# Ordering the splitting of weights behind the instructions that empty PSUM

## The chip, the cores and the metric

The kernel runs on one core of one Trainium2 chip. The metric is the device time of one execution in microseconds (us). Three runs of the kernel before took 2464.74, 2468.38 and 2469.51 us; their median is 2468.38. One more execution was recorded by the profiler, and all times inside the kernel come from that one.

TensorE (PE) multiplies matrices, VectorE (DVE) and ScalarE (ACT) work on tiles elementwise, SyncE (SP) issues the transfers. Each works through a queue of its own in order; engines wait for one another by semaphores.

## The reference

One layer of a streaming encoder for 256 frames of width 2048, in float32: a gated feed-forward block, a mixer of two attentions, a cross attention to 256 memory tokens with 4 heads of width 512, and a second feed-forward block. Each is followed by a layer norm of the scaled input plus the block's output. Cut to what matters here:

```python
def swiglu_ffn(x, w_in, w_out):
    g, u = jnp.split(x @ w_in, 2, axis=-1)
    return (jax.nn.silu(g) * u) @ w_out

def hybrid_mixer(u, ...):
    proj = u @ w_in                      # q, k, v of A; latents of B; two gates
    y_a = chunked_relbias_attention(q_a, k_a, v_a, rel_bias) @ w_o_a   # 16 heads of 64
    y_b = mla_attention(q_lat, kv_lat, ..., cos, sin) @ w_o_b          # 16 heads, rotary part
    return (g_a * y_a + g_b * y_b) @ w_out

def memory_cross_attention(h, mem, ...):
    k, v = split((layer_norm(mem) @ w_xkv))
    return softmax((h @ w_xq) @ k.T / sqrt(512)) @ v @ w_xo
```

Nearly all of the work is matrix products of 256 rows with large weights, each of which is read from memory once.

## The kernel before, in words

**Two halves.** Every float32 operand is split in two parts that TensorE multiplies at its faster format: hi, a rounded copy, and lo, the rest. A product is hi by both halves of the input plus lo by its hi half. For weights this is done on the chip: a raw weight tile of 128 x 2048 comes by one transfer of 1 MB (line 191), ScalarE rounds it in two casts of 1024 columns (`halves`, line 262), and VectorE subtracts (line 265). There are three buffers each for raw, hi and lo. Inputs are split the same way (lines 253 and 254).

**Units.** `run` walks a list of units, each of which multiplies one weight tile. Before it writes the instructions of unit i, it writes loading and splitting for the weights ahead, up to `UNITS` = 2 units ahead. The order in which the instructions finally stand in each engine's queue is made by the scheduler, which goes by priorities (mostly the order of writing) and by what an instruction depends on; `issue_after(x)` adds that an instruction stands behind x in its engine's queue.

**What empties PSUM.** There are four banks for results of the kind `mm` and four of the kind `at`. A wide unit (`mm_wide`, lines 275 and 277) has 16 matmuls of hi into 512 columns and 16 of lo into 256. Its result is added up by `total`: ScalarE copies the upper half (line 283), VectorE adds the lower (line 284). The feed-forward blocks and the larger projections (line 309, and line 363 for those with sums of weights, which lines 246 and 248 form on VectorE) use a scheme with fewer products, whose results are combined by `shared`: two copies on ScalarE (lines 674 and 675) and four operations on VectorE (676 to 679).

**Softmax.** In the attentions VectorE adds the bias (line 1055) and finds the maxima (824), ScalarE takes exponentials (827), VectorE normalizes (831). The result is transposed by a transfer: ScalarE sorts the bytes into planes (841), SP issues the transfer, ScalarE joins the planes again (849). `join` has the order "behind `next_hi`", the last cast of the next weight. Lines 1028 and 1082/1083 are the scores and the outputs of an attention; 973 scales a transposed input.

Of the kernel before, what the change touches and what calls it, by code (L numbers as in the profile page):

```python
# [14 lines left out]
ALU = mybir.AluOpType  # L15
# [4 lines left out]
S = 256  # L20
# [53 lines left out]
class Act:  # L74


    def __init__(self, blocks):
        self.blocks = blocks
# [21 lines left out]
class Kernel:  # L100
    def __init__(self, ctx, tc, t, out):
        self.tc, self.nc, self.t, self.out = tc, tc.nc, t, out

        def pool(name, bufs=1, **kw):
            return ctx.enter_context(tc.tile_pool(name=name, bufs=bufs, **kw))

        self.const = pool("const")
        self.wraw = pool("wraw", 3)
        self.whi = pool("whi", UNITS + 1)
        self.wlo = pool("wlo", UNITS + 1)  # L110
        self.blocks = pool("blocks")
        self.res = pool("res")
        self.work = pool("work", 4)
        self.small = pool("small", 4)
        self.ps_mm = pool("ps_mm", 4, space=PSUM)
        self.ps_at = pool("ps_at", 4, space=PSUM)
        self.items = []
        self.uid = 0
        self.chain = self.sent = self.last_hi = self.ln_act = None
        self.cut = self.early = False  # L120


    def name(self, s):
# [128 lines left out]
    def split(self, src, hi, lo):  # L252
        copied = self.nc.scalar.copy(hi, src)
        self.nc.vector.tensor_tensor(lo, src, hi.bitcast(F32), ALU.subtract)
        return copied

    def halves(self, src, hi, lo):

        n = src.shape[1]
        for c in range(0, n, 1024):  # L260
            d = min(c + 1024, n)
            self.last_hi = self.nc.scalar.copy(hi[:, c:d], src[:, c:d])  # L262

        with self.tc.issue_after(self.chain.ins) if self.chain is not None else nullcontext():
            self.last_lo = self.nc.vector.tensor_tensor(lo[:, :n], src, hi[:, :n].bitcast(F32), ALU.subtract)  # L265
        return hi, lo

# [11 lines left out]
    def total(self, ps, out=None, scale=1.0):  # L279

        t = self.w1()
        if scale == 1.0:
            self.nc.scalar.copy(t, ps[:, S:])
            self.nc.vector.tensor_tensor(t if out is None else out, t, ps[:, :S], ALU.add)  # L284
        else:
            self.nc.scalar.mul(t, ps[:, S:], scale)
            self.nc.vector.scalar_tensor_tensor(t if out is None else out, ps[:, :S], scale, t, ALU.mult, ALU.add)
        return t

    def mm_tok(self, ps, tt, w, x, kts, start, stop, c=0, m=512):  # L290
# [325 lines left out]
    def out_pair(self, bank, src, g, nk, x, at, fx, scale, st, sums_in=SUM_HOME):  # L616

        nc, h = self.nc, self.h
        ps, qs = {}, {}

        def shared():
            for (tt, a), s in qs["add"].items():
                c = (2 * g + a) * 512
                hs = h[tt][:, c:c + 512]
                if scale:
                    nc.vector.scalar_tensor_tensor(hs, hs, ALPHA, s, ALU.mult, ALU.add)
                else:
                    nc.vector.tensor_tensor(hs, hs, s, ALU.add)

        def finish():  # L630
            for tt in range(2):
                for a in range(2):
                    self.finish(tt, 2 * g + a, ps[tt, a], scale and not at, st)
        self.pair_group(bank, src, 512, nk, x, at, fx, ps, qs, shared, sums_in)
        self.add(finish)
# [33 lines left out]
    def shared(self, qs, n):  # L669

        nc = self.nc
        a, b, u, c = (self.w2()[:, :n] for _ in range(4))
        q = [qs[i][:, :n] for i in range(4)]
        nc.scalar.copy(a, q[0])
        nc.scalar.copy(b, q[1])
        nc.vector.tensor_tensor(u, a, q[2], ALU.add)
        nc.vector.tensor_tensor(b, b, u, ALU.subtract)
        nc.vector.tensor_tensor(u, u, q[3], ALU.add)
        nc.vector.tensor_tensor(c, b, q[3], ALU.subtract)  # L679
        qs["add"] = {(0, 0): a, (0, 1): b, (1, 0): u, (1, 1): c}  # L680

    def first_group(self, tag, xT, before, ps, fx):
# [1088 lines left out]
```

## Time and profile before

| | us |
|---|---|
| median of three runs | 2468.38 |
| lowest, highest run | 2464.74, 2469.51 |
| the profiled execution | 2465.43 |
| its span (first to last instruction) | 2463.7 |
| TensorE busy | 2430.7 |
| VectorE busy | 2121.4 |
| ScalarE busy | 1545.9 |

The profiled execution is 1.7 us longer than its span and 2.95 us below the median of the runs. In the lines of the waits, an engine, line and tile wait for another engine's line; behind the colon stand the sum in us, how many times, and the longest. In the timeline a row has the start, the duration of the group, the engine, line, operation and tiles, the number of instructions in the group (x), and in brackets how long the engine was idle before and what ended it. Rows of the windows have, for each engine, busy us and instructions in that stretch, and then the granted clock of TensorE, the share of the transfer engines in use, and GB/s. Instructions on an engine overlap a little: from one start to the next is some 0.1 us less than the duration.

### The profile page before, as it was taken

The page shows a single profiled execution, that of the slowest core. Times are in us where ns is not written, and L with a number is a line of the kernel's source. Part 1 is how long each engine was busy: PE and PEld are TensorE (multiplying, and loading weights), DVE is VectorE, ACT ScalarE, POOL GpSimd, SP SyncE. Part 2 cuts the span into 40 slices and gives each one's busy share as a digit, 9 for nine tenths or more (in the row PEclk, how much of TensorE's full clock was granted, in tenths as well). Part 3 has the DMA queues.
Part 4 walks back from the last instruction along what each step waited for, and adds up shares of the span by engine and source line. Part 5 has one row for each costly group of instructions (what it writes and reads, how often), then busy time and mean ns, then how long its engine had stood idle before and what let it go on. Part 6 is the DMA issues. An engine that isn't in the chain of part 4 may idle for free.

```text
span 2463.7 us, 29637 instructions
## 1 busy us (share of the span) xinstructions
PE 2430.7 (99%) x11286; PEld 2028.2 (82%) x11286; DVE 2121.4 (86%) x2423; ACT 1545.9 (63%) x2017; POOL 36.2 (1%) x81
## 2 busy tenths in 40 slices
PE   9999999999999999989999999999999999999999
PEld 8888888888888888878888887888888888887887
DVE  8999989889788897689788789869879999888896
ACT  6676655667455557778565686656566665556662
POOL 0000000000000001000000000000000000000000
PEclk9999999999999999999999999999999999999999
DMA  7766665656646656676676567555556666566564
GB/s 262 253 218 216 203 212 209 221 193 216 233 169 214 213 205 207 221 198 183 206 250 228 180 219 227 196 175 206 188 196 212 220 212 219 206 213 214 179 229 163
DMA packets 176415, 516.20 MB, mean 210 GB/s; under 512 B 111728, under 2 KB 112496, under 8 KB 121104
## 3 DMA queue, kind: packets, MB, share of 16 engines
q1 hardware_dynamic: 170816, 495.83, 59.8%
q0 software_dynamic: 4592, 17.30, 2.3%
q8 instruction: 88, 1.44, 0.2%
q10 hardware_dynamic: 864, 1.18, 0.1%
q14 instruction: 55, 0.45, 0.1%
HBM read 485.30 MB, written 2.10 MB: 198 GB/s over the span
## 4 chain that ended last, share of the span: by engine, by line
PE 74%; DVE 9%; ACT 8%; DMA 5%; issue 3%; SPq 0%; DVEq 0%; ACTq 0%
PE at L309 21%; PE mm L309 20%; PE mm L363 8%; PE at L363 8%; PE mm L296 8%; PE mm L275 4%; DVE lo L265 3%; ACT hi L262 3%; DMA raw<-ffn_w_in 2%; PE mm L277 2%; ACT w L849 1%; PE at L1028 1%; ACT X L262 1%; DMA raw<-w_xv 1%; DMA w<-w 0%
## 5 line engine op out<-in xcount | busy, mean ns | idle before, releaser
L262 ACT CAST hi<-raw 128x1024 fp32r<-128x1024 f32 (+1 forms) x852 | 804.3, 982 | 540.0 <-PE at L309 113.9
L265 DVE TENSOR_TENSOR lo<-raw,hi 128x2048 fp32r<-128x2048 f32 (+1 forms) x427 | 902.6, 2115 | 174.0 <-ACT hi L262 163.1
L309 PE MATMUL mm<-hi,T 128*128 128x512 f32 (+1 forms) x1328 | 311.7, 385 | 5.8 <-DVE w L679 4.6
L309 PEld LDWEIGHTS mm<-hi,T 128*128 128x128 f32 x1328 | 247.2, 188 | 54.8 <-DVE w L679 6.5
L309 PE MATMUL at<-hi,T 128*128 128x512 f32 x1152 | 275.4, 390 | 0.6 <-DVE w L679 0.6
L309 PEld LDWEIGHTS at<-hi,T 128*128 128x128 f32 x1152 | 215.8, 188 | 47.2 <-DVE w L679 2.4
L265 DVE TENSOR_TENSOR X<-H,X 128x2048 fp32r<-128x2048 f32 (+1 forms) x83 | 186.7, 2250 | 37.7 <-ACT X L262 37.7
L262 ACT CAST X<-H 128x1024 fp32r<-128x1024 f32 (+1 forms) x166 | 169.7, 1034 | 74.5 <-DVE H L248 48.0
L309 PE MATMUL mm<-lo,T 128*128 128x512 f32 (+1 forms) x664 | 160.6, 384 | 0.0
L309 PEld LDWEIGHTS mm<-lo,T 128*128 128x128 f32 x664 | 124.5, 189 | 23.1
L309 PE MATMUL at<-lo,T 128*128 128x512 f32 x576 | 142.6, 389 | 0.0
L309 PE MATMUL at<-hi,H 128*128 128x512 f32 x560 | 133.4, 390 | 0.1
L309 PEld LDWEIGHTS at<-lo,T 128*128 128x128 f32 x576 | 108.1, 188 | 22.4
L309 PE MATMUL mm<-hi,H 128*128 128x512 f32 x480 | 118.6, 398 | 6.1 <-DVE w L284 3.1
L309 PEld LDWEIGHTS at<-hi,H 128*128 128x128 f32 x560 | 104.9, 188 | 22.2 <-DVE w L679 0.6
L248 DVE TENSOR_TENSOR H<-H,raw 128x512 f32<-128x512 f32 (+1 forms) x166 | 112.4, 677 | 1.6
L309 PEld LDWEIGHTS mm<-hi,H 128*128 128x128 f32 x480 | 91.5, 192 | 26.6 <-DVE w L679 4.2
L246 DVE TENSOR_TENSOR H<-raw 128x1024 f32<-128x1024 f32 (+1 forms) x83 | 99.6, 1200 | 1.7 <-DMA raw<-ffn_w_in 0.9
L363 PE MATMUL mm<-X,X 128*128 128x512 f32 x342 | 90.2, 389 | 0.0
L262 ACT CAST X<-raw 128x1024 fp32r<-128x1024 f32 (+1 forms) x54 | 54.9, 1034 | 56.3 <-DVE raw L248 25.8
L363 PE MATMUL at<-X,X 128*128 128x512 f32 (+1 forms) x315 | 82.1, 385 | 3.5 <-ACT X L262 3.5
L849 ACT COPY w<-w 128x1024 uint16<-128x1024 uint16 (+1 forms) x60 | 73.6, 1270 | 7.3 <-DMA w<-w 7.3
(373 smaller groups left out, 4120.0 us busy)
## 6 DMA issues: line engine op xcount, KB each, us to landing
raw<-ffn_w_in SPq DMA_DIRECT2D x150, 1024.0 KB, 4.9
raw<-ffn_w_out SPq DMA_DIRECT2D x66, 1024.0 KB, 4.9
raw<-w_gate SPq DMA_DIRECT2D x32, 1024.0 KB, 4.8
raw<-ffn_w_out_r SPq DMA_DIRECT2D x16, 1024.0 KB, 5.1
raw<-w_qk SPq DMA_DIRECT2D x16, 1024.0 KB, 5.5
raw<-w_o_b SPq DMA_DIRECT2D x16, 1024.0 KB, 4.8
raw<-w_out SPq DMA_DIRECT2D x16, 1024.0 KB, 5.5
raw<-w_xk SPq DMA_DIRECT2D x16, 1024.0 KB, 5.5
```

What stands on the lines that cost most here:

```text
L246: self.nc.vector.tensor_tensor(two[0], two[1], raw[:, :m].unsqueeze(1).to_broadcast([P, 2, m]), ALU.add)
L248: self.nc.vector.tensor_tensor(t[:, a * m:a * m + m], t[:, b * m:b * m + m], raw[:, a * m:a * m + m], ALU.add)
L262: self.last_hi = self.nc.scalar.copy(hi[:, c:d], src[:, c:d])
L265: self.last_lo = self.nc.vector.tensor_tensor(lo[:, :n], src, hi[:, :n].bitcast(F32), ALU.subtract)
L275: self.nc.tensor.matmul(ps, hi[j], x.both(kt), start=(j == 0), stop=False)
L277: self.last_mm = self.nc.tensor.matmul(ps[:, :S], lo[j], x.at(0, kt), start=False, stop=(j == n - 1))
L296: self.last_mm = self.nc.tensor.matmul(ps, x.at(xi, kt)[:, tt * P:(tt + 1) * P], w[wi][:, j * 512 + c:j * 512 + c + m], start=(start and j ...
L309: self.last_mm = self.nc.tensor.matmul(ps[tt, g][:, :n], x.at(xi, kt)[:, tt * P:(tt + 1) * P], w[wi][:, c:c + n], start=first and j + wi + ...
L363: self.last_mm = self.nc.tensor.matmul(bank[:, :m], a[xi], v[wi][:, c * m:(c + 1) * m], start=own and first and wi + xi == 0, stop=own and ...
L849: self.nc.scalar.copy(self.words(u, n).rearrange("p (c k) -> p k c", k=2), self.words(s, n).rearrange("p (k c) -> p k c", k=2))
L1028: nc.tensor.matmul(ps[:, c0:c0 + nk], q[:, tt * P:(tt + 1) * P], k[:, :nk], start=(j == 0), stop=(j == len(parts) - 1))
```

## The change

`total` and `shared` now remember their last ScalarE and VectorE instruction (`evicted`). `halves` puts the two casts behind the remembered ScalarE instruction, and the subtraction behind the remembered VectorE instruction, in these engines' queues. No instruction is added, removed or altered. The lines of the helpers move: a cast of a weight is line 268 after, a subtraction 272, the copy and add of a total 290 and 291, the four steps of `shared` 684 to 687, the join 857.

```diff
@@ -118,6 +118,7 @@
         self.uid = 0
         self.chain = self.sent = self.last_hi = self.ln_act = None
         self.cut = self.early = False
+        self.evicted = {}
 
 
     def name(self, s):
@@ -254,14 +255,20 @@
         self.nc.vector.tensor_tensor(lo, src, hi.bitcast(F32), ALU.subtract)
         return copied
 
+    def after_out(self, engine):
+        last = self.evicted.get(engine)
+        return self.tc.issue_after(last.ins) if last is not None else nullcontext()
+
     def halves(self, src, hi, lo):
 
         n = src.shape[1]
-        for c in range(0, n, 1024):
-            d = min(c + 1024, n)
-            self.last_hi = self.nc.scalar.copy(hi[:, c:d], src[:, c:d])
-
-        with self.tc.issue_after(self.chain.ins) if self.chain is not None else nullcontext():
+        with self.after_out("act"):
+            for c in range(0, n, 1024):
+                d = min(c + 1024, n)
+                self.last_hi = self.nc.scalar.copy(hi[:, c:d], src[:, c:d])
+
+        with self.after_out("dve"), (
+                self.tc.issue_after(self.chain.ins) if self.chain is not None else nullcontext()):
             self.last_lo = self.nc.vector.tensor_tensor(lo[:, :n], src, hi[:, :n].bitcast(F32), ALU.subtract)
         return hi, lo
 
@@ -280,11 +287,12 @@
 
         t = self.w1()
         if scale == 1.0:
-            self.nc.scalar.copy(t, ps[:, S:])
-            self.nc.vector.tensor_tensor(t if out is None else out, t, ps[:, :S], ALU.add)
+            a = self.nc.scalar.copy(t, ps[:, S:])
+            d = self.nc.vector.tensor_tensor(t if out is None else out, t, ps[:, :S], ALU.add)
         else:
-            self.nc.scalar.mul(t, ps[:, S:], scale)
-            self.nc.vector.scalar_tensor_tensor(t if out is None else out, ps[:, :S], scale, t, ALU.mult, ALU.add)
+            a = self.nc.scalar.mul(t, ps[:, S:], scale)
+            d = self.nc.vector.scalar_tensor_tensor(t if out is None else out, ps[:, :S], scale, t, ALU.mult, ALU.add)
+        self.evicted = {"act": a, "dve": d}
         return t
 
     def mm_tok(self, ps, tt, w, x, kts, start, stop, c=0, m=512):
@@ -672,11 +680,11 @@
         a, b, u, c = (self.w2()[:, :n] for _ in range(4))
         q = [qs[i][:, :n] for i in range(4)]
         nc.scalar.copy(a, q[0])
-        nc.scalar.copy(b, q[1])
+        last = nc.scalar.copy(b, q[1])
         nc.vector.tensor_tensor(u, a, q[2], ALU.add)
         nc.vector.tensor_tensor(b, b, u, ALU.subtract)
         nc.vector.tensor_tensor(u, u, q[3], ALU.add)
-        nc.vector.tensor_tensor(c, b, q[3], ALU.subtract)
+        self.evicted = {"act": last, "dve": nc.vector.tensor_tensor(c, b, q[3], ALU.subtract)}
         qs["add"] = {(0, 0): a, (0, 1): b, (1, 0): u, (1, 1): c}
 
     def first_group(self, tag, xT, before, ps, fx):
```

The scheduler sorts the whole program anew round these edges. Three places in the queues follow. In them `mm_` and `at_` are PSUM tiles, `w_` work tiles, `raw_`, `hi_` and `lo_` a weight's tiles; numbers tell the tiles apart.

VectorE, at the end of the first attention's projections and the start of the rotary ones. `w_1216` and `w_1221` are the totals of the last two units, lines 1055/1063 and 824/832 the bias and maxima of a softmax. Before:

```order
L284 TENSOR_TENSOR w_1216_8034<-w_1216_8034,mm_8001 128x256
L265 TENSOR_TENSOR lo_8087<-raw_8084,hi_8086 128x2048
L265 TENSOR_TENSOR lo_8190<-raw_8187,hi_8189 128x2048
L1055 SCALAR_TENSOR_TENSOR w_1228_8105<-at_8102,X_1077_7102 128x384
L1055 SCALAR_TENSOR_TENSOR w_1232_8120<-at_8117,X_1077_7102 128x384
L824 TENSOR_REDUCE sm_m_8107<-w_1228_8105 128x1 x2
L824 TENSOR_REDUCE sm_m_8122<-w_1232_8120 128x1
L825 TENSOR_SCALAR sm_m_8107<-sm_m_8107 128x2
L824 TENSOR_REDUCE sm_m_8122<-w_1232_8120 128x1
L284 TENSOR_TENSOR w_1221_8081<-w_1221_8081,mm_8048 128x256
```

After:

```order
L291 TENSOR_TENSOR w_1216_8034<-w_1216_8034,mm_8001 128x256
L272 TENSOR_TENSOR lo_8040<-raw_8037,hi_8039 128x2048
L291 TENSOR_TENSOR w_1221_8081<-w_1221_8081,mm_8048 128x256
L1063 SCALAR_TENSOR_TENSOR w_1228_8105<-at_8102,X_1077_7102 128x384
L832 TENSOR_REDUCE sm_m_8107<-w_1228_8105 128x1 x2
L1063 SCALAR_TENSOR_TENSOR w_1232_8120<-at_8117,X_1077_7102 128x384
L833 TENSOR_SCALAR sm_m_8107<-sm_m_8107 128x2
L272 TENSOR_TENSOR lo_8087<-raw_8084,hi_8086 128x2048
L832 TENSOR_REDUCE sm_m_8122<-w_1232_8120 128x1 x2
```

The second total `w_1221` stood last, behind two subtractions and the start of a softmax; it now stands directly behind the subtraction `lo_8040`, which was further up, and `lo_8190` is further down.

VectorE, at the combination of the first query of the cross attention. Before:

```order
L265 TENSOR_TENSOR lo_11947<-raw_11944,hi_11946 128x2048
L265 TENSOR_TENSOR lo_11977<-raw_11974,hi_11976 128x2048
L676 TENSOR_TENSOR w_1856_11983<-w_1854_11981,mm_11796 128x512
L677 TENSOR_TENSOR w_1855_11982<-w_1855_11982,w_1856_11983 128x512
L265 TENSOR_TENSOR lo_12018<-raw_12015,hi_12017 128x2048
L678 TENSOR_TENSOR w_1856_11983<-w_1856_11983,mm_11797 128x512
L679 TENSOR_TENSOR w_1857_11984<-w_1855_11982,mm_11797 128x512
L1452 TENSOR_TENSOR w_1854_11981<-w_1854_11981,at_11717 128x512
```

After:

```order
L272 TENSOR_TENSOR lo_11947<-raw_11944,hi_11946 128x2048
L272 TENSOR_TENSOR lo_11977<-raw_11974,hi_11976 128x2048
L684 TENSOR_TENSOR w_1856_11983<-w_1854_11981,mm_11796 128x512
L685 TENSOR_TENSOR w_1855_11982<-w_1855_11982,w_1856_11983 128x512
L686 TENSOR_TENSOR w_1856_11983<-w_1856_11983,mm_11797 128x512
L687 TENSOR_TENSOR w_1857_11984<-w_1855_11982,mm_11797 128x512
L272 TENSOR_TENSOR lo_12018<-raw_12015,hi_12017 128x2048
L1460 TENSOR_TENSOR w_1854_11981<-w_1854_11981,at_11717 128x512
```

The subtraction `lo_12018`, which stood between the second and the third step of `shared`, stands behind the fourth.

ScalarE, at the first outputs of the first attention. `w_1106` and `w_1107` are the two halves of the first pair's softmax, whose joins the first output needs. Before:

```order
L841 COPY w_1106_7315<-w_1099_7288 128x768
L283 COPY w_1109_7352<-mm_7319 128x256
L841 COPY w_1107_7317<-w_1103_7303 128x768
L262 CAST hi_7412<-raw_7410 128x1024 x2
L262 CAST hi_7502<-raw_7500 128x1024 x2
L283 COPY w_1116_7407<-mm_7374 128x256
L849 COPY w_1106_7315<-w_1099_7288 128x2x384
L849 COPY w_1107_7317<-w_1103_7303 128x2x384
```

After:

```order
L857 COPY X_1068_7054<-H_1060_7023 128x2x512
L857 COPY w_1106_7315<-w_1099_7288 128x2x384
L981 ACTIVATE X_1114_7363<-X_1068_7054,vecs 128x256 x4
L849 COPY w_1128_7460<-w_1121_7433 128x768
L290 COPY w_1131_7497<-mm_7464 128x256
L268 CAST hi_7502<-raw_7500 128x1024 x2
L857 COPY w_1107_7317<-w_1103_7303 128x2x384
L849 COPY w_1129_7462<-w_1125_7448 128x768
L290 COPY w_1136_7544<-mm_7511 128x256
```

The two joins stood together behind the copy of `w_1116`. Now the first stands ahead of four scalings and the second behind those, the planes `w_1128`, the copy of `w_1131` and the casts of `hi_7502`.

## The prediction

> **What bounds the kernel now.** I began with the first part of the page (span, busy time), then the waits of TensorE, then the timeline round its longest waits, and last the windows for the granted clock.
>
> ```profile
> span 2463.7 us, 29637 instructions
> PE 2430.7 (99%) x11286; PEld 2028.2 (82%) x11286; DVE 2121.4 (86%) x2423; ACT 1545.9 (63%) x2017; POOL 36.2 (1%) x81
> ...
> PE mm L275 <- DVE w L284: 7.7, 2, 7.3
> PE mm L309 <- DVE w L679: 7.5, 6, 2.9
> PE at L363 <- ACT X L262: 3.5, 5, 1.2
> PE mm L309 <- DVE w L284: 3.1, 1, 3.1
> ...
> PE at L309 <- DVE w L679: 0.6, 3, 0.2
> ```
>
> TensorE idles 2463.7 − 2430.7 = 33.0 us in all. No change of order can win more than that and what a low clock costs behind the idle times. Of the 33.0, 7.7 + 7.5 + 3.1 + 0.6 = 18.9 us are waits for two kinds of VectorE instruction: the last step of a total (L284) and of a shared combination (L679), which empty PSUM banks. These are just what the change orders against the weights' roundings (ACT L262) and low halves (DVE L265).
>
> ```profile
> 469.00:475.00 6.00, 5.42 (x24) 4.49 (x25) 6.00 (x9) 4.23 (x6) 0.00 (x0) 1.00 0.36 147
> 1060.00:1066.00 6.00, 5.94 (x20) 5.00 (x21) 3.34 (x14) 5.18 (x14) 0.00 (x0) 0.60 0.28 58
> 1521.00:1527.00 6.00, 5.25 (x16) 4.16 (x17) 6.00 (x9) 4.67 (x5) 0.00 (x0) 0.72 0.42 79
> 1527.00:1533.00 6.00, 6.00 (x28) 4.97 (x27) 5.49 (x9) 3.41 (x5) 0.00 (x0) 1.00 0.97 330
> ...
> 2234.00:2240.00 6.00, 5.89 (x19) 4.71 (x20) 5.92 (x9) 3.99 (x5) 0.00 (x0) 0.72 0.29 122
> ```
>
> The third number from the end is the granted clock. Behind the waits that end at 1060, 1521 and 2234 it is 0.60, 0.72 and 0.72, though TensorE is nearly always busy there: 6 × 0.40 = 2.4 and 6 × 0.28 = 1.7 us of work are lost. The neighbour of 1521 runs 28 matmuls at 1.00, the disturbed stretch 16. For the wait of 3.13 that ends at 1621, I take the same 1.7. Behind the 1.48 us wait that ends at 469.58 the clock stays 1.00. So a long wait costs about two microseconds more than itself, and a short one does not.
>
> [...]
>
> **The change, part by part.** Nothing is added or taken away: the same casts (about 1 us per half), subtractions (2.2 us from start to start) and copies run, in another order. The new edges lie within one engine's queue, so none adds a wait between engines. I therefore cost each place by what stands ahead of the PSUM instruction before and after.
>
> *(a) The rope projections, span time 1060.*
>
> ```profile
> 1053.34 1.98 ACT L262 CAST hi<-raw 128x1024 fp32r<-128x1024 f32 x2
> 1055.22 0.36 ACT L283 COPY w<-mm 128x256 f32<-128x256 f32 x1
> 1055.35 2.29 DVE L265 TENSOR_TENSOR lo<-raw,hi 128x2048 fp32r<-128x2048 f32 x1 [1.51 <-ACT hi L262]
> 1059.59 0.42 DVE L284 TENSOR_TENSOR w<-w,mm 128x256 f32<-128x256 f32 x1
> 1060.06 1.22 PE L275 MATMUL mm<-X,hi 128*128 128x512 f32 x2 [7.33 <-DVE w L284]
> ```
>
> The copy stands behind two casts, the add behind a subtraction and a softmax, while all four mm banks are full. In the new order the add of this total comes before that softmax and that subtraction. Following the new queue with these durations, the projections that had to wait run on until one of the second four, which wants the next total: about 0.9 us stays. Gain: of 7.33 and a 0.41 us wait just ahead (the two of the first row of waits, 7.7), 6.8; plus the clock behind it, 2.3 (from the window, 2.4): **9.1**. From below: if a bank frees only after the next subtraction, 2.2 less. What is late next would be the latent keys' weights; hi and lo of the first are made by the two rows of 1053.34 and 1055.35, before this stall ends, so TensorE finds them ready.
>
> *(b) The first query's combination, 1521.*
>
> ```profile
> 1518.21 2.29 DVE L265 TENSOR_TENSOR lo<-raw,hi 128x2048 fp32r<-128x2048 f32 x1
> 1520.42 0.68 DVE L678 TENSOR_TENSOR w<-w,mm 128x512 f32<-128x512 f32 x1
> 1521.75 0.50 PE L309 MATMUL mm<-hi,H 128*128 128x512 f32 x1 [2.85 <-DVE w L679]
> ```
>
> In the new order the four steps stand together and the subtraction behind them: 1520.42 − 1518.21 = 2.2 of the 2.85 goes, 0.65 stays, and that is under the wait of 1.48 that cost no clock, so 1.7 more: **3.9**.
>
> *(c) The end of the keys, 1621.*
>
> ```profile
> 1611.20 3.82 PE L275 MATMUL mm<-H,hi 128*128 128x512 f32 x16
> ...
> 1616.77 1.78 PE L309 MATMUL mm<-hi,H 128*128 128x512 f32 x7
> 1618.76 1.99 ACT L262 CAST hi<-raw 128x1024 fp32r<-128x1024 f32 x2
> 1620.65 0.37 ACT L283 COPY w<-mm 128x256 f32<-128x256 f32 x1
> 1621.21 0.41 DVE L284 TENSOR_TENSOR w<-w,mm 128x256 f32<-128x256 f32 x1
> 1621.68 3.65 PE L309 MATMUL mm<-hi,H 128*128 128x512 f32 x9 [3.13 <-DVE w L284]
> ```
>
> The unit of this total begins at 1611.20 and ends when the row of 1616.77 begins; the copy could start then. In the new order it does, about 1617.0, and the add follows by 1617.8, while the seven matmuls last until 1618.5. All 3.13 goes, and 1.7 of clock: **4.8**.
>
> *(d) and (e) The feed-forward combinations.*
>
> ```profile
> 469.58 0.73 PE L309 MATMUL mm<-hi,T 128*128 128x512 f32 x2 [1.48 <-DVE w L679]
> ...
> 2229.37 2.29 DVE L265 TENSOR_TENSOR lo<-raw,hi 128x2048 fp32r<-128x2048 f32 x1
> 2232.17 0.69 DVE L248 TENSOR_TENSOR H<-H,raw 128x512 f32<-128x512 f32 x1
> 2234.11 1.20 PE L309 MATMUL mm<-hi,T 128*128 128x512 f32 x4 [2.32 <-DVE w L679]
> ```
>
> Here the scheduler fills the gap again: the subtraction (2.2) and one sum L248 (0.6) leave the four steps, two such sums (1.2) come between them. Net 1.6: 2234 keeps 0.7 of 2.32 and loses its 1.7 of clock, **3.3**; 469 loses its 1.48, and the smaller waits for L679 (7.5 − 2.85 − 2.32 − 1.48 = 0.9, and 0.6 in the other row, in all 1.5) are counted at 1.2: **2.7**.
>
> *(f) A new wait, at the first attention output.* Each join of a transposed softmax (L849) is itself ordered behind the next weight's cast, so a later cast takes it along; the second join of the first pair now stands behind the casts of a further weight.
>
> ```profile
> 968.95 0.93 PE L1028 MATMUL at<-w,w 64*128 64x128 f32 x8
> ...
> 970.97 2.00 ACT L262 CAST hi<-raw 128x1024 fp32r<-128x1024 f32 x2
> 973.14 2.59 ACT L849 COPY X<-H 128x1024 uint16<-128x1024 uint16 x2
> 975.76 1.71 ACT L973 ACTIVATE X<-X,vecs 128x256 fp32r<-128x256 f32 x4
> 977.49 1.28 ACT L827 ACT_TABLE_LOAD   x1
> 978.78 0.40 ACT L827 ACTIVATE w<-w,sm_m 128x128 f32<-128x128 f32 x1
> 980.59 0.83 ACT L841 COPY w<-w 128x768 uint16<-128x768 uint16 x1
> 986.39 2.00 ACT L849 COPY w<-w 128x768 uint16<-128x768 uint16 x2
> 993.37 0.66 PE L1082 MATMUL at<-w,H 128*64 128x256 f32 x4
> ```
>
> Before, both joins end at 988.4, five microseconds early. After, I lay the new queue's rows end to end, by the distance from each start to the next, from the copy of the total whose unit ends where the first row begins, 969.0. Up to the end of the second join there are four copies of totals (4 × 0.27 = 1.1), four pairs of casts (4 × 1.9 = 7.6), four joins of the large transposes (4 × 1.25 = 5.0), eight scalings (2 × 1.7 = 3.4), the table load (1.3), two softmaxes' exponentials (2 × 1.8 = 3.6), three planes (3 × 0.75 = 2.2) and the two joins themselves (2 × 0.95 = 1.9). The sum is 26.1, the end 995.1. TensorE wants it in the second half of the row of 993.37 and its like, at 993.8: a wait of **1.3**. Bounds: 0, if some of it is over earlier, and with the rows' full durations 3.7 and 1.7 of clock.
>
> *(g) Thinner cover.* A weight's cast now waits for the total of the unit before the last, so hi and lo are made one unit ahead instead of two. A wide unit lasts 1616.77 − 1611.20 = 5.6 us, and lo is wanted only 3.8 us after it begins (its first row). So the wide stages hide this: a copy, two casts and a subtraction are 0.3 + 1.9 + 2.2 = 4.4 us. Thin places are the feed-forward's sums of weights (the five waits of L363, 3.5) and the cross keys; I put **1.0**, with bounds 0 and 6 (one more wait of 1.2 at each of five groups).
>
> Sum: 9.1 + 3.9 + 4.8 + 3.3 + 2.7 − 1.3 − 1.0 = 21.5. The profiled execution took 2465.43 us; the median of the runs is 2.95 above it. So 2465.43 − 21.5 + 2.95 = **2446.9**.
>
> **Rivals.**
>
> *Half comes back.* A place freed runs into the next late thing: a w_xv load behind 1617, a sums unit behind 469 or 2234, the softmax behind 1052. For it: ScalarE and VectorE are the emptiers and the makers, and VectorE is 86% busy. Against: no row of TensorE's waits above names hi or lo of an ordinary weight, so these are ahead of it now. Half of the sum is a gain of 10: 2458.
>
> *The lookahead was needed.* One mechanism: ScalarE's copy waits for TensorE, and the casts now queue behind it, so a stage in which ScalarE has more than about 3 us of other work per 5.5 us unit delivers hi late, in every unit.
>
> ```profile
> 1410.00:1420.00 10.00, 10.00 (x57) 8.71 (x56) 7.01 (x8) 10.00 (x15) 0.00 (x0) 1.00 1.07 366
> ```
>
> In the cross keys ScalarE has no gap while TensorE is still full. If the eight key units there and the sixteen of the first attention were each late by the 1.3 of (f), that is 24 × 1.3 = 31; less the gains (a) to (e), 23.8, about 7 slower, 2476. Against: following the new queue through the cross keys, I find hi still in time, if by little, because nearly the same instructions precede it there.
>
> *The change does not do what it says* where it matters: the adds wait for ScalarE's copies rather than for the subtractions, and the scheduler puts other work between them as in (d). Then only (b) and (c) hold, less (f) and (g), about 6: 2462; or nothing: 2468.
>
> **How the numbers follow.** My sum 0.60; half comes back 0.20 (0.16 of it still faster by over 0.2%, 0.04 the same); it does little 0.10 (0.04 faster, 0.06 same); lookahead 0.10 (0.08 slower, 0.02 same). 0.2% of the time, 4.9 us, is about what a measurement of this kernel can tell from no change. Faster 0.80, same 0.12, slower 0.08. For the range: the most is (a) to (e) with no loss, 23.8, and another 4 if the thinner waits shrink too: 2440. Upwards (f) and (g) at their bounds take 4 + 5 = 9, with (a) 2.2 short 2458; the half case and part of the third carry it to 2465. So 2440 to 2465; my sum's own range is 2441 to 2456.
>
> **What would show it.** The row of waits of totals from the wide projections falls from 7.7 to about 1; those for combinations from 7.5 to under 2.5; that of L309 on a total is gone; the granted clock is 1.00 at 1521, 1617 and 2230 and at the rope; a new wait of an attention output (L1082, by its new line) on the join of about 1.3 appears; TensorE idles some 19 us instead of 33. The forecast is wrong if waits of matmuls on hi or lo appear in the key stages, if the clock dips at new places, or if the idle time falls without the time doing so.

## The result

The changed kernel took 2448.6 us (median of 4 runs, 2446.28 to 2450.31), beside 2467.09 for the kernel before (now the median of 4 runs): a ratio of 0.9924, 95% interval 0.9907 to 0.9942. In a later series it took 2447.87 beside 2464.64, 0.9931 (0.9918 to 0.9943). It is faster by 18.5 and 16.8 us. 2446.9 had been forecast, a gain of 21.5 from 2468.38.

The profiled execution took 2450.02 us. The page's first part, span and TensorE's busy time:

```profile
span 2448.0 us, 29669 instructions
...
PE 2425.6 (99%) x11286; PEld 2026.6 (83%) x11286; DVE 2122.2 (87%) x2423; ACT 1547.5 (63%) x2017; POOL 36.1 (1%) x81
```

TensorE idles 22.4 us instead of 33.0, and is busy for 5.1 less: together the 15.7 us by which the span fell. The granted clock was low in four places before (0.60 at 1060, 0.72 at 1521, 1621 and 2234), which cost 2.4 + 3 x 1.7 = 7.5 us of work, and in two after (0.72 at 962 and 1539), 3.4 us; that is 4.1 of the 5.1. TensorE's waits after (sum, how many, longest):

```profile
PE at L371 <- ACT X L268: 6.2, 5, 2.2
PE at L371 <- DVE X L272: 2.4, 1, 2.4
PE mm L284 <- DVE lo L272: 1.9, 1, 1.9
...
PE at L1090 <- ACT w L857: 0.8, 1, 0.8
...
PE mm L317 <- DVE w L687: 0.6, 1, 0.6
PE at L1090 <- ACT T L857: 0.3, 1, 0.3
```

The waits for totals, 7.7 and 3.1, are gone. Those for combinations fell from 8.1 to 0.6. In their place stand larger waits for the half X of a sum of weights (by its cast 6.2 instead of 3.5, by its subtraction 2.4), one for a weight's low half (1.9), and the join's 0.8 + 0.3.

The windows behind these places, with the granted clock third from the end:

```profile
962.00:968.00 6.00, 5.82 (x26) 5.35 (x27) 3.92 (x6) 2.27 (x3) 0.00 (x0) 0.72 0.83 210
1056.00:1062.00 6.00, 5.96 (x34) 5.04 (x33) 3.75 (x12) 5.76 (x13) 0.00 (x0) 1.00 0.94 255
1512.00:1518.00 6.00, 5.38 (x24) 4.21 (x23) 6.00 (x8) 3.63 (x5) 0.00 (x0) 1.00 0.00 0
1539.00:1545.00 6.00, 5.42 (x17) 4.37 (x18) 6.00 (x6) 4.28 (x5) 0.00 (x0) 0.72 0.39 161
1617.00:1623.00 6.00, 5.32 (x34) 4.48 (x33) 5.25 (x6) 3.09 (x6) 0.00 (x0) 1.00 0.54 188
2218.00:2224.00 6.00, 6.00 (x29) 4.95 (x28) 6.00 (x8) 2.81 (x5) 0.00 (x0) 1.00 0.43 150
```

At the four old places (rope, first query, end of the keys, feed-forward) the clock is 1.00. It is 0.72 at two new ones, 962 and 1539.

**The place at 1539.** First the rows after, from the timelines of ScalarE, VectorE and TensorE; then the same work before.

```profile
1534.90 1.05 ACT L268 CAST X<-T 128x1024 fp32r<-128x1024 f32 x1
1535.03 2.29 DVE L272 TENSOR_TENSOR lo<-raw,hi 128x2048 fp32r<-128x2048 f32 x1
1537.24 2.28 DVE L272 TENSOR_TENSOR X<-T,X 128x2048 fp32r<-128x2048 f32 x1
1539.58 1.65 PE L371 MATMUL at<-X,T 128*128 128x512 f32 x3 [2.38 <-DVE X L272]
```

```profile
1541.34 2.29 DVE L265 TENSOR_TENSOR lo<-raw,hi 128x2048 fp32r<-128x2048 f32 x1
1543.55 2.29 DVE L265 TENSOR_TENSOR X<-T,X 128x2048 fp32r<-128x2048 f32 x1
...
1547.08 0.84 PE L363 MATMUL at<-X,T 128*128 128x512 f32 x3
```

VectorE's order is the same in both: the next weight's low half, then X. Before, X ended at 1545.84, 1.2 us ahead of its use. After, TensorE would want X at 1537.2, 9.9 us earlier than before, but VectorE comes to these two rows only 6.3 us earlier, and X ends at 1539.52. The difference, 3.6, less the 1.2 that were in hand, is the wait. VectorE works there without a gap from 1527.08 on. That it is step (b), won just ahead, which brings TensorE there too soon is tried below.

**The place at 962.** After, on ScalarE, VectorE and TensorE; then VectorE before.

```profile
953.04 2.00 ACT L268 CAST hi<-raw 128x1024 fp32r<-128x1024 f32 x2
953.17 0.42 DVE L291 TENSOR_TENSOR w<-w,mm 128x256 f32<-128x256 f32 x1 [2.66 <-ACT w L290]
959.17 0.42 DVE L1008 TENSOR_TENSOR w<-w,w 128x256 f32<-128x256 f32 x1 [5.57 <-DMA w<-w]
959.51 0.42 DVE L1009 TENSOR_TENSOR w<-w,w 128x256 f32<-128x256 f32 x1
959.85 2.28 DVE L272 TENSOR_TENSOR lo<-raw,hi 128x2048 fp32r<-128x2048 f32 x1
...
962.18 3.49 PE L284 MATMUL mm<-T,lo 128*128 128x256 f32 x16 [1.87 <-DVE lo L272]
```

```profile
954.24 2.29 DVE L265 TENSOR_TENSOR lo<-raw,hi 128x2048 fp32r<-128x2048 f32 x1
957.32 0.42 DVE L1000 TENSOR_TENSOR w<-w,w 128x256 f32<-128x256 f32 x1 [0.79 <-DMA w<-w]
```

The low half is that of the third weight of the first attention's queries and keys (`w_qk`); the expectations below call it the second latent key weight. Before, it stood ahead of the rotation of the shared key (L1000 before, L1008 and L1009 after), which waits for a transfer that swaps the key's rows. After, its hi is cast behind a total's copy and is ready at 955.04, and the scheduler has put the rotation between the total at 953.17 and the low half. VectorE stands still for 5.57 us, and the low half comes 1.87 us too late.

### The profile page after: what moved, and what is told of

Read it like the earlier page. It is cut to its first block, busy times and chain, and to the rows that moved or that the text cites. A ratio compares the mean times of both kernels' runs of the same rounds, so it can differ in the third digit from the quotient of the medians.

```text
span 2448.0 us, 29669 instructions
## 1 busy us (share of the span) xinstructions
PE 2425.6 (99%) x11286; PEld 2026.6 (83%) x11286; DVE 2122.2 (87%) x2423; ACT 1547.5 (63%) x2017; POOL 36.1 (1%) x81
## 4 chain that ended last, share of the span: by engine, by line
PE 79%; DVE 8%; ACT 6%; DMA 4%; issue 2%; SPq 0%; POOL 0%; DVEq 0%; ACTq 0%
PE at L317 23%; PE mm L317 20%; PE at L371 10%; PE mm L371 9%; PE mm L304 9%; PE mm L282 3%; DVE lo L272 3%; ACT hi L268 2%; PE mm L284 2%; DMA raw<-w_xv 1%; PE at L1036 1%; DMA raw<-ffn_w_in 1%; ACT H L849 0%; DMA raw<-ffn_w_in_r 0%; PE at L282 0%
## 5 line engine op out<-in xcount | busy, mean ns | idle before, releaser
L317 PEld LDWEIGHTS at<-lo,T 128*128 128x128 f32 x576 | 108.1, 188 | 22.4
L272 DVE TENSOR_TENSOR X<-raw,X 128x2048 fp32r<-128x2048 f32 (+1 forms) x27 | 60.5, 2248 | 17.5 <-ACT X L268 17.5
```

Of the source, the lines that this page charges most:

```text
L317: self.last_mm = self.nc.tensor.matmul(ps[tt, g][:, :n], x.at(xi, kt)[:, tt * P:(tt + 1) * P], w[wi][:, c:c + n], start=first and j + wi + ...
```

## The experiments

All are made from the changed kernel, except the one that says so. Each was timed beside the kernel before on the same chip. The expected times start from 2448.6 and 2467.1; on the chips of these runs the kernel before took 2463.7, 2461.9 and 2464.6, so the last two columns are what to compare.

| kernel | median | less the kernel before | ratio, 95% interval |
|---|---|---|---|
| only totals hold back | 2451.33 | -12.4 | 0.9951 (0.9938 to 0.9964) |
| only combinations hold back | 2457.22 | -6.5 | 0.9971 (0.9961 to 0.9982) |
| only subtractions are held back | 2451.11 | -12.6 | 0.9945 (0.9933 to 0.9958) |
| only casts are held back | 2448.63 | -15.1 | 0.9940 (0.9926 to 0.9953) |
| step (b) undone | 2447.10 | -14.8 | 0.9934 (0.9922 to 0.9946) |
| rotation later | 2443.44 | -18.5 | 0.9921 (0.9908 to 0.9933) |
| X first | 2439.07 | -22.9 | 0.9901 (0.9886 to 0.9916) |
| rotation later and X first | 2434.18 | -27.7 | 0.9885 (0.9871 to 0.9898) |
| the same once more | 2434.61 | -30.0 | 0.9879 (0.9864 to 0.9894) |
| the change once more | 2447.87 | -16.8 | 0.9931 (0.9918 to 0.9943) |
| both additions, casts' edge alone | 2440.27 | -24.4 | 0.9900 (0.9887 to 0.9914) |
| both additions, without the change | 2454.20 | -10.4 | 0.9958 (0.9945 to 0.9970) |

### Totals alone, combinations alone

```diff
# only totals: in shared()
-        self.evicted = {"act": last, "dve": nc.vector.tensor_tensor(c, b, q[3], ALU.subtract)}
+        self.evicted = {}
+        nc.vector.tensor_tensor(c, b, q[3], ALU.subtract)
# only combinations: in total()
-        self.evicted = {"act": a, "dve": d}
+        self.evicted = {}
```

> Only the totals hold back the weights' casts and subtractions; the combinations do so no longer (steps (a) and (c) alone). Theory, that the gains were of the predicted size and the losses came from thinner cover: (a) 10.4 and (c) 4.7 remain, the waits at 469, 1521 and 2234 come back, and of the losses stay the 1.87 us wait of the second latent key weight at 962 with its 1.7 of clock, and the join, about 1: 2467.1 - 15.1 + 4.6 = 2456.6. The wait of 2.38 at 1539 should be gone, since the combination at 1521 is late again. Rival, that the losses come from the combinations: then 962 is undisturbed and the time is about 2452.

> Only the combinations hold back the weights' casts and subtractions; the totals do so no longer (steps (b), (d), (e) alone). Theory: gains 3.9 + 3.8 + 3.7 = 11.4, losses at 1539 of 4.4 and at the feed-forward's sums of about 3: 2467.1 - 4 = 2463, with the wait of 7.3 at the rope and the 3.1 at the end of the keys back in place, and no wait at 962. Rival, that the losses come from the totals: 2467.1 - 11.4 = 2456.

12.4 where 10.5 was expected, 6.5 where 4 was; their sum, 18.9, is about the whole change's 16.8 to 18.5, as it would be if the two halves worked at separate places. From TensorE's waits with totals alone (one line further down in the code), then with combinations alone:

```profile
PE mm L317 <- DVE w L688: 6.2, 7, 2.5
...
PE mm L284 <- DVE lo L272: 1.9, 1, 1.9
```

```profile
PE mm L282 <- DVE w L291: 8.0, 2, 7.6
...
PE at L371 <- DVE X L272: 2.4, 1, 2.4
```

With totals alone the rope is repaired, the wait at 962 (1.9) is there and the one of 2.4 on X is not; with combinations alone it is the other way round. This settles where each loss comes from: 962 belongs to the totals and 1539 to the combinations, as both theories had it, so by the waits neither rival holds.

### Subtractions alone, casts alone

```diff
# only subtractions are held back: in halves()
-        with self.after_out("act"):
+        with nullcontext():
# only casts are held back: in halves()
-        with self.after_out("dve"), (
+        with nullcontext(), (
```

> Only VectorE's subtractions stand behind the sums and combinations; ScalarE's casts are free of them. If what counts at the rope and at the end of the keys is ScalarE's copy behind two casts, then (c) is not had at all and (a) at most by half, while (b), (d) and (e) are had whole and the losses at 962 and 1539 stay: about 2461. Rival, that the subtraction alone was the block: 2449 as the whole change, or better by the join's 1 us.

> Only ScalarE's casts stand behind the sums' and combinations' copies; VectorE's subtractions are free of them. By the same theory (c) comes by about 3 of 4.7, (a) by at most 3, and (b), (d), (e) not at all, less 1 for the join; no wait of 2.38 at 1539: about 2462. Rival, that the casts alone were the block: 2449 to 2452.

Both expectations fail. The casts' edge alone brings 15.1 of the whole 16.8 to 18.5, where 5 was expected; the rival, that the casts alone were the block (15 to 18), fits. The subtractions' edge alone brings 12.6 where 6 was. These overlap: the sum is 27.7. At the rope with casts alone, from the timelines of ScalarE, VectorE and TensorE:

```profile
1053.71 0.65 ACT L290 COPY w<-mm 128x256 f32<-128x256 f32 x2
...
1055.56 0.74 DVE L291 TENSOR_TENSOR T<-w,mm 128x256 f32<-128x256 f32 x2
...
1056.02 1.19 PE L282 MATMUL mm<-X,hi 128*128 128x512 f32 x4
1057.11 1.05 ACT L268 CAST hi<-raw 128x1024 fp32r<-128x1024 f32 x1
```

No cast stands ahead of the copies, and since a low half needs its hi, no subtraction stands ahead of the adds either: holding back the cast holds back the subtraction, without an edge of its own. So TensorE does not wait there. With subtractions alone:

```profile
1050.09 0.74 PE L284 MATMUL mm<-X,lo 128*128 128x256 f32 x4 [2.41 <-DVE lo L272]
...
1053.58 2.28 DVE L272 TENSOR_TENSOR lo<-raw,hi 128x2048 fp32r<-128x2048 f32 x1
...
1058.22 0.41 DVE L291 TENSOR_TENSOR T<-w,mm 128x256 f32<-128x256 f32 x1
...
1058.68 1.19 PE L282 MATMUL mm<-X,hi 128*128 128x512 f32 x4 [2.11 <-DVE T L291]
```

Here the rope has 2.41 us for a low half and 2.11 for a total, 4.5 instead of 7.7. That (a) comes by half at most held; that nothing of (c) comes did not, since its wait fell from 3.13 to 1.38. What the casts' edge alone leaves standing, and the subtractions' edge would take, is 2.08 of (b) and 2.4 of small waits for combinations; the wait of 2.38 at 1539 is then only 0.42.

The wait at 962 comes with the casts' edge alone too:

```profile
959.65 0.43 DVE L1008 TENSOR_TENSOR w<-w,w 128x256 f32<-128x256 f32 x1 [5.45 <-DMA w<-w]
...
962.67 2.17 PE L284 MATMUL mm<-T,lo 128*128 128x256 f32 x16 [1.75 <-DVE lo L272]
```

With the subtractions alone VectorE also waits for that transfer, 5.65 us, with the low half behind it; but the transfer lands at 955.10, and TensorE does not wait. Why it lands sooner there was not shown.

### Is what (b) won given back at 1539?

```diff
+        self.calls = getattr(self, "calls", 0) + 1
+        if self.calls != 23:          # 23: the first cross query
+            self.evicted = {"act": last, "dve": d}
```

> The change with one exception: the combination of the first cross query (step (b)) no longer holds back the casts and subtractions that follow it. Theory, that what (b) won was given back at the next late sum, 1539: the wait of about 2.9 before the second query's matmuls returns, the one of 2.38 on a sum's half X disappears, and the time is 2447 to 2450, as with the whole change. Rival, that the two are unrelated: 2448.6 + 3.9 = 2452.5, both waits there.

The time cannot tell: 14.8 under the kernel before is what the rival expected (14.6), and the theory 17 to 20, but the interval, 0.9922 to 0.9946, spans both. The trace can. TensorE's waits have this row for combinations and none for the subtraction of an X of more than 0.4:

```profile
PE mm L317 <- DVE w L687: 2.5, 1, 2.5
```

With (b) TensorE waits 0.62 here and 2.38 at 1539, 3.0 in all; without (b) 2.5, once. One wait took the place of the other, as the theory said, and the rival that both stay is out by the waits.

### The rotation later, X first

```diff
# rotation later: kpe ends behind the swap; its three operations become krot()
-        a_proj(0)
+        a_proj(0, ((lambda: self.behind(krot),), ()))   # behind the low half then written last
# X first: run() remembers the subtraction of a sum's X; halves() goes behind it
+                self.sum_lo = self.last_lo
...
         with self.after_out("dve"), (
+                self.tc.issue_after(self.sum_lo.ins) if self.sum_lo is not None else nullcontext()), (
```

> The whole change, and the rotation of the shared key (two multiplications and an addition that wait 5.6 us for its swap transfer) is put behind the low half of the second latent key weight on VectorE. Theory: the wait of 1.87 at 962 on that low half and the half clock behind it go, 1.9 + 1.7 = 3.6: about 2445. Rival, that TensorE would next wait there for the following weight's half or total: 2447 to 2449.

> The whole change, and each weight's low half is put behind the subtraction of the preceding sum of weights (X) on VectorE. Theory: at 1539 X is formed 2.2 us earlier (2.29 us of an ordinary low half no longer ahead of it), the wait of 2.38 shrinks to 0.2 to 1.2 and its 1.7 of clock goes: 2445 to 2446; the waits at 117, 568 and 2321 stay, since there X is late by its sum and not by an ordinary low half. Rival, that the low half is then late itself, at 1545 and in the other sums: 2449 to 2452.

> Both additions together: the shared key's rotation behind the second low half, and the low halves behind the sums' subtraction. If the two losses are independent, their gains add: 3.6 + 3 = 6.6, about 2442, with no granted clock under 1.00 behind 962 and 1539. Rival, that a stretch won before 1539 runs into the next late piece: 2445.

With the rotation later, no matmul waits for a weight's low half any more. With both additions (the second time) the rotation waits 2.45 us for its transfer at 955.11, and the low half of 962, which stands ahead of it, ends at 952.66, well before TensorE's matmuls of it begin at 955.45. In the time the expected 3.6 does not show: 18.5 under the kernel before, as the change itself (18.5 and 16.8), where 22 was expected. Its profile still has the 2.38 of 1539, now at 1532, with a clock of 0.72 behind it (1532 to 1538), and a new low clock, 0.72 from 2315 to 2321.

X first brought 22.9, where 21 to 22 was expected: the wait at 1539 is 1.13, with full clock behind it (1.0 is the mean over the whole recorded execution), and the one at 962 grew to 2.83. The expectation that the waits at 117, 568 and 2321 would stay was wrong; they are gone. VectorE ahead of 568 in the changed kernel, then with both additions:

```profile
566.31 0.55 DVE L249 TENSOR_TENSOR H<-H,raw 128x384 f32<-128x384 f32 x1
566.78 1.75 DVE L272 TENSOR_TENSOR lo<-raw,hi 128x1536 fp32r<-128x1536 f32 x1
568.45 0.55 DVE L249 TENSOR_TENSOR H<-H,raw 128x384 f32<-128x384 f32 x1
```

```profile
561.19 1.15 DVE L251 TENSOR_TENSOR H<-H,raw 128x384 f32<-128x384 f32 x2
564.74 1.76 DVE L275 TENSOR_TENSOR X<-H,X 128x1536 fp32r<-128x1536 f32 x1 [2.40 <-ACT X L270]
566.41 1.75 DVE L275 TENSOR_TENSOR lo<-raw,hi 128x1536 fp32r<-128x1536 f32 x1
```

In the changed kernel an ordinary low half stands between the two last additions of the sum. Ordered behind X, it leaves the gap, and TensorE's two waits there, 1.23 and 0.49, go. The gap is not all of it: the 1.23 ended with a cast of X that began at 567.63, ahead of the second addition, and with both additions the first step of the sum comes at 559.05 instead of 564.17, while TensorE comes only 1.7 us earlier. What moved it so far was not shown.

Both together bring 27.7, where 25 was expected. The profile of both, the second time:

```profile
span 2432.4 us, 29630 instructions
...
PE 2420.4 (100%) x11286; PEld 2024.2 (83%) x11286; DVE 2119.0 (87%) x2423; ACT 1549.2 (64%) x2017; POOL 35.9 (1%) x81
```

TensorE idles 12.0 us. The longest wait left is 1.1, and the clock is 1.00 at 955 and at 1527, where the places of 962 and 1539 now lie.

### The change beside both additions, with and without

> The changed kernel as it is, once more, beside the next three on one chip: the ratio to the kernel before should again be 0.992, within 0.9907 to 0.9942. If the half clock behind waits of about two microseconds falls by chance (it was there behind waits of 1.87 and 1.81, and absent behind 2.37 and 2.83, at the same places in different kernels), the waits at 962, 1539 and 2321 return with their lengths, but the granted clock behind some of them differs from the first profile; if it is fixed by the place, 0.72 comes again at 962 and 1539 and 1.00 at 2321.

> The casts' edge, the rotation behind the second low half, and the low halves behind the sums' subtraction; no edge of VectorE on the totals and combinations. With the casts' edge alone the rope's wait was gone already, but the first query's combination kept 2.08 us and the small waits of combinations 2.4; if the subtractions' edge pays once its cost at 1539 is removed, this is slower than the kernel with both additions by 2 to 5 us: 2436 to 2439. Rival, that the subtractions' edge is worth nothing at any place: 2434.

> The two additions (rotation later, low halves behind the sums' subtraction) on the kernel before, without the change. Theory, that they repair places which the change made thin: they win only what the five waits of 3.5 us on a sum's half X hold, 0 to 4 us under the kernel before. Rival, that they are gains of their own: 9 to 10 us under it, as on top of the change.

> The change with both additions once more, on one chip with the change alone: 9 to 10 us under it (2434 against 2443 to 2444), ratio to the kernel before 0.9885 again. Rival, that the difference of the two ratios, 0.9924 and 0.9885, came from the chips: 5 us or less.

The edits are those shown: with casts alone `halves` loses `after_out("dve")`, and without the change `after_out` never returns an instruction. Four kernels on one chip, beside 2464.64: the change -16.8, the additions without it -10.4, both -30.0. The additions alone win 10.4, where the theory that they only mend what the change made thin had 0 to 4, so that theory is wrong. Both together win 2.8 more than the sum, which is no more than the runs of one kernel differ by. On this one chip they lie 13.3 under the change, where 9 to 10 was expected, so the gain did not come from the chips. The waits without the change:

```profile
PE mm L285 <- DVE w L294: 7.7, 2, 7.3
PE mm L320 <- DVE w L690: 3.0, 2, 2.8
...
PE at L374 <- DVE X L275: 0.8, 2, 0.5
```

Most of the five waits for X, 3.5, is gone, and so are the waits at 469 and 2234. At 469 the low half that stood between the first and second step of the combination is no longer there, since it is ordered behind an X. That is a second way to most of (d) and (e), though two waits for combinations, 2.4 in all, stand elsewhere. The rope's 7.7, the first query's 2.8 and the wait at the end of the keys (2.6) need the change.

With both additions the subtractions' edge is worth 2440.27 - 2434.61 = 5.7 us, a little over the expected 2 to 5: without it the wait at (b), 2.06 with a clock of 0.72 behind it (1507 to 1513), and 2.4 of small waits for combinations stand there.

The kernel with the change and both additions beats both kernels of this case: 2434.2 and 2434.6 us.

## Why the prediction was right, and where not

**What bounds it: right.** The idle time of TensorE (33.0 to 22.4 us) and the low clock behind it (7.5 to 3.4 us of work) make up 14.7 of the 15.7 us by which the span fell.

**(a) rope, 9.1: right, a little small.** The row of totals fell by 7.7, of which about 0.9 had been expected to stay, and the clock is 1.00: 7.7 + 2.4 = 10.1. The working gave the copy and the add equal weight; the run with casts alone shows that ordering the casts is enough there.

**(b) 3.9 and (c) 4.8: right.** (b): 2.85 fell to 0.62 and the clock is 1.00, 2.2 + 1.7. (c): the wait is gone, with its clock, 3.1 + 1.7; the 1.7 had been taken over from its neighbours, and the profile before has 0.72 from 1621 to 1627, which bears it out.

**(d) 3.3 and (e) 2.7: right, a little small.** No wait for a combination is left but that of (b): 2.32 + 1.7 = 4.0, and 1.48 + 1.5 = 3.0.

So the gains by rows are 10.1 + 3.9 + 4.8 + 4.0 + 3.0 = 25.8, against 23.8 predicted. The three 1.7s in them are those of one recorded execution; the last section shows that such a price is not paid every time.

**(f) the join, 1.3: right.** 0.8 + 0.3 = 1.1.

**(g) thinner cover, 1.0 with bounds 0 and 6: wrong, and the only term that was far off.** The rows give 2.7 (casts of X, 6.2 less 3.5), 2.4 + 1.7 at 1539 and 1.9 + 1.7 at 962: 10.4 us, beyond the upper bound. In the second recorded execution of the changed kernel the casts of X have 4.4 and the clock at 1539 is full: 0.9 + 2.4 + 1.9 + 1.7 = 6.9, beyond it too. The step looked for a low half or hi that comes late in a unit, and priced the sums of weights alone. Two mechanisms were missed:

- 962: copy, casts and subtraction were laid end to end, 4.4 us, by which the low half, from the copy at 952.77, would have been ready at 957.2, three microseconds ahead of its use at 960.3. What else would stand ahead of the subtraction in VectorE's queue was not looked at; the rotation, which waits for a transfer, stood there.
- 1539: a matmul that is no longer held back comes to its next operand sooner, while the engine that makes this operand, busy without a gap, gains less (6.3 us against 9.9). Slack ahead of the next operands was checked in the old timeline, not in the one with the gain in it. Before, X was 1.2 us early, less than the 3.9 that (b) wins.

25.8 less 10.4 and 1.1 is 14.3, beside the 15.7 by which the span fell; the rest are small waits. The medians fell by more, 18.5 and 16.8: the profiled execution of the changed kernel, 2450.02, lies near the top of its range, that of the kernel before, 2465.43, near the bottom; the second recorded span of the changed kernel is 2443.5, 20.2 less than before.

So it is partly luck that the time came within 1.7 us of the forecast. By the rows of the first pair of profiles the net gain is 14.3 and not 21.5; the gains were 2.0 larger than predicted, which hid a part of what (g) lacked; and the median of the kernel before fell by 1.3 with a fourth run, below the 2468.38 that the forecast started from. TensorE idles 22.4 us, not the 19 that had been named as a sign.

Of the rivals, "half comes back" named what happened at 1539, a freed place that runs into the next late thing, and by rows 11.5 of 25.8 did come back, not far from half. The time is still nearer to the forecast, 2446.9, than to that rival's 2458: the gains were 2 us larger than the sum it halved, and the medians fell by more than the profiled spans. "The lookahead was needed" is out: no unit of the cross keys or of the first attention but one, at 962, waits for hi or lo. "Does little" is out by the rope alone.

Two of the signs named for a wrong forecast came true all the same: a matmul of a key stage waits for a low half, and the clock dips at new places. They cost what (g) had left out.

## What to carry to other kernels

Begin with the first producer of a chain: the cast's edge drew the subtraction with it and brought most of the gain (15.1 of 16.8 to 18.5 us), and what the second edge adds (5.7 us with both additions) showed only once the places behind it were mended. When a wait is removed, go on to the next operand and ask by how much it was early, because the engine that makes it may have no gap to close: at 1539 TensorE came 9.9 us earlier, VectorE, busy throughout, only 6.3. And look in an in-order queue at what stands ahead of an instruction that is made later: if that waits for a transfer, both are held up, as by the 5.57 us at 962.

## What was not expected of the hardware

Taken microsecond by microsecond, the 0.72 behind 962 in the first profile is 0.78 from 962 to 963, 0.50 or 0.51 from 963 to 966, and 1.00 from 966 on. From the window it is a half clock for some 6 x 0.28 / 0.5 = 3.4 us, an estimate. In these runs the half clock behind a wait of some two microseconds follows neither from the length of the wait nor from the place. The windows behind 962 and 1539 in the second run of the changed kernel, where the waits were 1.94 and 2.38:

```profile
961.00:967.00 6.00, 6.00 (x28) 5.34 (x28) 4.45 (x6) 2.26 (x3) 0.00 (x0) 0.72 0.90 226
1537.00:1543.00 6.00, 6.00 (x27) 4.96 (x27) 6.00 (x6) 4.47 (x6) 0.00 (x0) 1.00 0.27 113
```

At 962 it is 0.72 both times; with totals alone it is 1.00 there (963 to 969), behind 1.95 us. At 1539 the clock was 0.72 in the first profile and 1.00 in this one, behind the same 2.38 us in the same program. The window behind a wait of 1.81 us, with one of 0.50 just after it, with the rotation later, and behind one of 2.83 us with X first:

```profile
2315.00:2321.00 6.00, 4.90 (x18) 4.58 (x19) 4.62 (x6) 5.97 (x9) 0.00 (x0) 0.72 0.79 300
```

```profile
959.00:965.00 6.00, 5.79 (x34) 5.15 (x35) 5.13 (x7) 2.27 (x3) 0.00 (x0) 1.00 0.83 209
```

It was halved behind the shorter and not behind the longer. The same goes for a place of the kernel before: behind (b)'s 2.85 us the clock was 0.72, and behind 2.81 us at that place in the kernel with the additions alone it is 1.00. So the 1.7 us that the prediction set behind each such wait is a price paid in some executions only, and a part of the scatter of a kernel's runs may be just this; that was not shown. The kernel with both additions, which has no wait over 1.1, scatters least: 2433.82 to 2436.05 and 2434.15 to 2434.97.

What brings the half clock about in one execution and not in another was not shown, and how much idle time it takes was not tried here.
